# The scan's products of the state in two row halves of TensorE, and the first phase's steps in another order

## The chip, the cores and the metric

The kernel runs on one core of a Trainium2 chip. The metric is the device time of one execution in microseconds, the median of three runs. One more execution was recorded by the profiler; all durations below come from that one.

## What is computed

One decoder layer over 520 columns: 512 tokens of one prompt and 8 single new tokens of 8 running sequences. Differential attention (prompt tokens among themselves, new tokens against a paged cache) and an RWKV-7 time mixing run side by side, gates merge them, and a dense feed-forward network follows. The part that the change touches is the recurrence of the time mixing over the prompt, for 8 heads with a 64x64 state each:

```python
def step(S, inp):
    r_t, w_t, k_t, v_t, kk_t, a_t = inp
    sa = jnp.einsum("bhij,bhj->bhi", S, -kk_t)
    S = (S * w_t[:, :, None, :] + sa[..., None] * (kk_t * a_t)[:, :, None, :]
         + v_t[..., None] * k_t[:, :, None, :])
    return S, jnp.einsum("bhij,bhj->bhi", S, r_t)
S_fin, y = lax.scan(step, wkv0.astype(f32), seq)
```

## The kernel before

All activations stand with channels on the 128 partitions and the 520 columns along the free axis. A **first phase** computes all projections, the time mixing, both attentions, the gates and the merged product of both branches. A **second phase** (output projection and feed-forward network, tile `psW`) follows; no line of it is changed.

Dense products keep 32-bit accuracy by splitting: `whi` (ScalarE, ACT) and `wlo` (VectorE, DVE) are made from each loaded weight block `raw`, and TensorE (PE) runs three products per block into `psD`. An ordinary 32-bit product, such as those of the scan, appears in the trace as two matmuls, so 8 products are 16 matmuls there.

The recurrence is done in 16 **chunks** of 32 tokens (`scan_chain`, two chunks `e` per call `p`). A chunk takes the state `old`, a tile `STB` of 128 partitions: the 64 key channels of the even heads stand in the upper row half, those of the odd heads in the lower one, and four pairs of heads lie along the free axis. Its chain of work is:

1. 8 products of the state, one per head, of `WZ` (64 columns for each head: 32 for the solved keys, 32 for the receptance) with `old`, into one PSUM bank of the tag `P`, named `psC`. Here the contraction runs over all 128 partitions, and `WZ` holds zeros in the row half of the other head of the pair.
2. DVE adds `u0` to the first 32 rows and writes `uv`; ACT copies the other 32 rows to `yg`, the output.
3. 8 products of `bt` and `uv` (contraction over 64 rows, heads alternating between two column halves) into a second tile, also named `psC`.
4. DVE adds the decayed old state `SD` and writes the new `STB`, and makes the next `SD`.

Everything else of the scan hangs beside this chain: `scan_w` loads and computes `WZ` of the next pair of chunks, `scan_ak` and `scan_u0` make `u0`, `scan_post` (products `psR<-uv,G`) completes the output. `solve` inverts the 32x32 triangles on DVE; it borrows both `WZ` tiles for its result and its scratch, and sets their padding halves to zero on GpSimd (POOL) afterwards.

The order of the first phase is not the order of the code. Each operation is recorded as a numbered step (`Steps`), and the table `SEQ` lists the numbers in the order in which they are issued; this sets the order on every engine's queue and on the DMA queues (SP for weights, cache pages and constants, ACT for most others). `BUFS` gives the number of buffers of the shared pools: 35 of `T2` (SBUF, 520 columns) and 8 of `P` (one PSUM bank each, all 8 that there are).

Of the kernel before, what the change touches and what calls it, by code (L numbers as in the profile page):

```python
# [20 lines left out]
TP = 512  # L21
# [34 lines left out]
def host_consts():  # L56
# [41 lines left out]
BUFS = {"Q4": 4, "T2": 35, "raw": 2, "w": 2, "P": 8}  # L98
SEQ = """
    708 3 76 639 72 0 19 1873 14 73 9 5 1943 34 1874 24 39 29 642 2 4 63 1 71 640 65 64 643 77 67-68 62 20 641 57 22  # L100
    66 58 21 56 15 59 10 711 16 60 12 11 74 6 4445 35 7-8 36 644-655 25 136 61 13 40 26 17 669-680 41 30 18 27 31-32
    37 23 681-692 42 139 28 78 710 33 70 656-667 69 79 38 82-93 80 43 81 44 50 45 107-118 51 46 52 47 94-105 53 48
    75 54 49 55 119-130 668 138 140 693 106 694 141 695-698 142 131 700 144-155 699 143 133 701 134 132 169-180 135
    137 214 212 215 208 213 226 574 198 510 209 200 199 156-167 201 181-192 575 168 576 202 193 577 195 579-590 578
    203 197 287 227 196 702 194 604-615 429 222 591-602 511-512 616-627 603 703-704 216-219 628 228 629-630 229 210
    220-221 206 211 204 207 631 205 257-268 223 632 232-243 705 224 706-707 633 709 515-526 225 230 634 231 540-551
    635 288 1870 1867 636 244-255 513 637 514 638 269-280 256 349 552-563 281 289 283 290 282 527-538 284 564 419
    285 430 293-304 291 539 565 286 566 292 420 348 318-329 421-422 305-316 423 352 424 330-341 353 317 425 414-415
    342 350 426 344 567 351 343 409-410 416 345 417 427 418 354-365 712-713 568 1029 346 411 437 428 569 366-377 431
    413 412 434 570 432 478 433 379-390 571 347 378 572 391-402 436 714 573 715 1314 716 403 506 404 1312 405 1315  # L110
    998 717 996 1313 835 1013 999 1316 997 1011 1317 406 1000 718-729 1014 1318 1012 1001 407 1319 915 1002 1320 408
    1015 743-754 1321 1003-1005 1322 1006 1017 1323-1325 1007 730-741 1016 1008 1018 1326 1019 1030 1009 1020
    1327-1329 742 1010 1031 773 834 755-766 1330 435 1021 438 1034-1045 481 767 1032 769 1033 1059-1070 768 770 774
    771 916 905 1046-1057 772 836-837 906 1058 1028 1071-1082 907-908 900-901 909 1083 1085 840-851 910 838 911
    865-876 902 839 903-904 912 1084 1151 852-863 923 775 913 776 877-888 914 479 482 864 922 895-896 921 777 889
    779-790 1087 778 891 1086 897 1710 898 1088 804-815 899 893 890 917 892 918 791-802 919 1152 894 1153 816-827
    803 1181-1192 828 1154 830 1155 829 1022-1023 831 1090 1193-1204 1024 832 924 920 968 965 992 439-446 964
    925-932 1205 833 1221 1150 944-951 1206 1089 1362 447-454 967 963 952-959 455 933-940 960 458-465 457 966 456
    941 466-473 962 1156-1167 474 961 477 943 942 476 1168-1179 480 1091 475 483-486 1092 1713 488-491 1180 487
    1120-1131 1714 492 1207 1095-1106 493 1208-1210 986-989 1093 993 990 1094 974-977 991 994 1363 1132-1143 978 995  # L120
# [172 lines left out]
def body(ctx, tc, A):  # L293
# [396 lines left out]

    STB = [c1.tile([128, 4, 64], F32, name=f"STB{i}") for i in range(2)]

    WZ = [c1.tile([128, 2, 4, 2, 2, 32], F32, name=f"WZ{i}") for i in range(2)]

    def solve():
        au = TT.rearrange("p g h t -> p (g h) t")
# [732 lines left out]
```

## Time and profile before

| | |
|---|---|
| median of 3 runs | 934.95 us (933.47 to 935.07) |
| the profiled execution, its own time | 939.28 us |
| its span, first to last instruction | 937.5 us |
| PE busy | 902.8 us, 96% of the span |
| DVE busy | 566.7 us, 60% |
| ACT busy | 408.3 us, 44% |
| granted TensorE clock, mean | 0.996 |

PE is the busiest engine in every stretch. The first product of the first phase starts at 9.6 us, the first of the second phase at 511 us. Chunk 0 of the scan starts at 247 us, and the products of the state of the last chunk run at 383 us. A busy share of PE says that a matmul was in flight, and matmuls overlap: two that start 60 ns apart can each last 220 ns. So the cost of a group of matmuls is read from the time that the group occupies, not from the sum of durations.

### The profile page before, as it was taken

What the parts mean: (1) busy time and instruction counts of PE and PEld (TensorE: products, weight loads), DVE (VectorE), ACT (ScalarE), POOL (GpSimd) and SP (SyncE); (2) the same over time, 40 slices, a digit from 0 to 9 for tenths busy, and PEclk for the clock granted to TensorE, in tenths of its full rate; (3) what the DMA queues carried; (4) which work ended last, traced back from release to release, by engine and by line L of the source; (5) the groups of instructions that cost most, each with busy time, mean ns of one, the idle gap of its engine ahead of it and who ended that gap; (6) DMA issues with size and microseconds to landing.
All of it is one profiled execution on the core that took longest, in us unless ns stands there. A gap on an engine that the chain in (4) does not pass through costs nothing.

```text
span 937.5 us, 20851 instructions
## 1 busy us (share of the span) xinstructions
PE 902.8 (96%) x8419; PEld 846.2 (90%) x8419; DVE 566.7 (60%) x1179; ACT 408.3 (44%) x863; POOL 61.7 (7%) x85
## 2 busy tenths in 40 slices
PE   5999999989999989999999999999999999999998
PEld 5798989888786768789999999999999999999998
DVE  5467767778455797663467666566666655533332
ACT  8565455543465633313444446444444444322221
POOL 1000201100000177000000000000000000000000
PEclk9999999999999999999999999999999999999999
DMA  7132346745827777778963222222233222243432
GB/s 235 63 104 69 103 125 187 204 153 183 222 64 261 219 247 244 235 278 280 299 220 128 91 90 91 91 91 90 91 98 103 92 90 92 85 113 108 114 106 63
DMA packets 78867, 136.46 MB, mean 146 GB/s; under 512 B 20289, under 2 KB 33473, under 8 KB 78770
## 3 DMA queue, kind: packets, MB, share of 16 engines
q1 hardware_dynamic: 45438, 110.75, 37.0%
q10 hardware_dynamic: 33332, 24.38, 8.7%
q8 instruction: 66, 1.08, 0.5%
q14 instruction: 31, 0.25, 0.1%
HBM read 117.86 MB, written 17.23 MB: 144 GB/s over the span
## 4 chain that ended last, share of the span: by engine, by line
PE 75%; DMA 8%; DVE 2%; ACT 2%; SPq 1%; issue 1%; ACTq 1%; DVEq 0%
PE psW L277 45%; PE psD L277 21%; PE psR L277 4%; PE psB L277 2%; PE psA L277 2%; DMA vt<-cache_v 2%; DMA kt<-cache_k 2%; DMA raw<-w_in 1%; PE psC L277 1%; DVE wlo L277 1%; ACTq L277 1%; DMA raw<-w_pab 1%; DMA uv<-vtd 1%; SPq L1005 1%; ACT es L277 1%
## 5 line engine op out<-in xcount | busy, mean ns | idle before, releaser
L277 ACT CAST whi<-raw 128x512 fp32r<-128x512 f32 x252 | 154.0, 613 | 385.2 <-PE psW L277 240.0
L277 DVE TENSOR_TENSOR wlo<-raw,whi 128x512 fp32r<-128x512 f32 x252 | 174.1, 692 | 215.0 <-ACT whi L277 209.9
L277 PE MATMUL psD<-X,whi 128*128 128x260 f32 x1344 | 260.7, 294 | 9.8 <-ACT X L277 9.6
L277 PEld LDWEIGHTS psD<-X,whi 128*128 128x128 f32 x1344 | 211.3, 191 | 23.5 <-issue 9.7
L277 PE MATMUL psW<-F,whi 128*128 128x348 f32 (+1 forms) x1056 | 223.8, 320 | 0.0
L277 PE MATMUL psD<-X,wlo 128*128 128x260 f32 x672 | 191.9, 286 | 1.1 <-DVE wlo L277 0.9
L277 PEld LDWEIGHTS psW<-F,whi 128*128 128x128 f32 x1056 | 163.4, 188 | 0.1
L277 PE MATMUL psW<-F,wlo 128*128 128x260 f32 x704 | 140.4, 281 | 0.0
L277 PEld LDWEIGHTS psD<-X,wlo 128*128 128x128 f32 x672 | 128.2, 191 | 2.0 <-DVE wlo L277 1.9
L277 PEld LDWEIGHTS psW<-F,wlo 128*128 128x128 f32 x704 | 121.2, 188 | 0.3 <-DVE wlo L277 0.3
L277 PE MATMUL psW<-HH,whi 128*128 128x348 f32 x528 | 111.8, 320 | 0.0
L277 PEld LDWEIGHTS psW<-HH,whi 128*128 128x128 f32 x528 | 81.6, 188 | 0.0
L277 PE MATMUL psW<-HH,wlo 128*128 128x260 f32 x352 | 70.3, 280 | 0.0
L277 PEld LDWEIGHTS psW<-HH,wlo 128*128 128x128 f32 x352 | 60.7, 188 | 0.0
L277 PE MATMUL psW<-M,whi 128*128 128x348 f32 (+1 forms) x192 | 40.8, 320 | 0.6 <-ACT whi L277 0.6
L277 DVE TENSOR_TENSOR X<-psW,X 128x348 f32<-128x348 f32 (+1 forms) x64 | 24.3, 422 | 14.2 <-PE psW L277 14.1
L277 PEld LDWEIGHTS psW<-M,whi 128*128 128x128 f32 x192 | 29.7, 188 | 0.8 <-ACT whi L277 0.8
L277 PE MATMUL psW<-M,wlo 128*128 128x260 f32 x128 | 25.6, 281 | 0.0
L277 DVE TENSOR_TENSOR pc<-psD,RSTD 128x260 f32<-128x260 f32 x28 | 12.0, 427 | 20.1 <-PE psD L277 20.0
L277 PE MATMUL psB<-vt,ptm 128*8 128x128 f32 x512 | 17.0, 273 | 5.6 <-DMA vt<-cache_v 4.2
L277 PEld LDWEIGHTS psW<-M,wlo 128*128 128x128 f32 x128 | 22.1, 188 | 0.0
L277 PEld LDWEIGHTS psB<-vt,ptm 128*8 128x8 f32 x512 | 12.3, 89 | 9.5 <-DMA vt<-cache_v 6.2
(319 smaller groups left out, 1230.2 us busy)
## 6 DMA issues: line engine op xcount, KB each, us to landing
raw<-w_in SPq DMA_DIRECT2D x42, 512.0 KB, 4.4
kt<-cache_k SPq DMA_DIRECT2D x64, 256.0 KB, 4.0
vt<-cache_v SPq DMA_DIRECT2D x64, 256.0 KB, 3.6
raw<-w_gate SPq DMA_DIRECT2D x22, 512.0 KB, 3.2
raw<-w_up SPq DMA_DIRECT2D x22, 512.0 KB, 3.2
raw<-w_down SPq DMA_DIRECT2D x16, 512.0 KB, 3.4
gad<-gt ACTq DMA_DIRECT2D x16, 260.0 KB, 3.7
raw<-w_pab SPq DMA_DIRECT2D x8, 512.0 KB, 6.3
```

The costliest lines, as they stand in the source:

```text
L277: return self.steps.add(self.name, op, roots, lambda: getattr(self.eng, op)(*map(real, a), **{k: real(v) for k, v in kw.items()}))
L1005: return nc.sync.dma_start(out=t[:, i, :].get(), in_=src[bass.ds(v, 1)].rearrange("o p c -> (o p) c"))
```

## The change

The products of the state no longer contract over zeros. The even head of a pair is contracted over the upper 64 rows, the odd one over the lower 64 rows, each with its own part of `WZ`. They write the same 64 PSUM partitions, and for that the result `sc` now has two banks, one for each parity; these two banks are a tag of their own (`PP`, one buffer), and `P` goes from 8 buffers to 6. The two readers of `sc` go through both banks with a rearranged view (`by_half`).

`WZ` becomes one tile with two halves, one for each `p % 2`, of the size of one of the two tiles before. One DMA fills a half where two did; one ACT copy of 128 partitions takes the place of two of 64; the zeroing in `solve` is gone, and the scratch of `solve` is now a `T2` tile, of which there are 36.

The table `SEQ` is another one from its first entry on, and the order changes throughout the first phase.

```diff
-BUFS = {"Q4": 4, "T2": 35, "raw": 2, "w": 2, "P": 8}
+BUFS = {"Q4": 4, "T2": 36, "raw": 2, "w": 2, "P": 6}
 SEQ = """
-    708 3 76 639 72 0 19 1873 14 73 9 5 1943 34 1874 24 39 29 642 2 4 63 1 71 640 65 64 643 77 67-68 62 20 641 57 22
...
-    WZ = [c1.tile([128, 2, 4, 2, 2, 32], F32, name=f"WZ{i}") for i in range(2)]
+    WZ = c1.tile([128, 2, 4, 2, 2, 32], F32, name="WZ")
...
-        rr = WZ[1].rearrange("p a h e i t -> p (a h e i t)")
+        rr = WZ.rearrange("p a h e i t -> p (a h e i t)")
...
-        tmpr = WZ[0].rearrange("p a h e i t -> p (a h e i t)")
+        tmpr = T2("R", "tmpr")
...
-        for t in WZ:
-            for i in range(2):
-                pool.memset(t[64 * (1 - i):64 * (1 - i) + 64, i], 0.0)
...
-        wr = WZ[p % 2]
-        for i in range(2):
-            q = slice(64 * i, 64 * i + 64)
-            act.dma_start(out=wr[q, i].rearrange("p h e i t -> p h (e i t)"), in_=wrd[p, q])
+        wr = WZ[:, p % 2]
+        act.dma_start(out=wr.rearrange("p h e i t -> p h (e i t)"), in_=wrd[p])
...
-            for i in range(2):
-                q = slice(64 * i, 64 * i + 64)
-                act.copy(out=wr[q, i, :, e, 0, :], in_=ps[q])
+            act.copy(out=wr[:, :, e, 0, :], in_=ps)
...
-                sc = PS("C")
+                sc = late(psp, [128, 2, 512], F32, "PP", 1, "sc")
                 for h in range(8):
-                    pe.matmul(out=sc[r0:r0 + 64, h * 64:h * 64 + 64], lhsT=wr[:, h % 2, h // 2, e, :, :], rhs=old[:, h // 2, :],
+                    q, a = slice(64 * (h % 2), 64 * (h % 2) + 64), h // 2
+                    pe.matmul(out=sc[r0:r0 + 64, h % 2, a * 64:a * 64 + 64], lhsT=wr[q, a, e, :, :], rhs=old[q, a, :],
                               start=True, stop=True)
-                dve.tensor_tensor(out=uv[r0:r0 + 32, :TP], in0=sc[r0:r0 + 32, :], in1=u0[w0:w0 + 32, :], op=ALU.add)
-                act.copy(out=yg[b0 + 32 * e:b0 + 32 * e + 32, :TP], in_=sc[r0 + 32:r0 + 64, :])
+
+                def by_half(x):
+                    return x.rearrange("p (a b j) -> p b a j", b=2, j=64)
+
+                sv = sc[:, :, :256].rearrange("p b (a j) -> p b a j", j=64)
+                dve.tensor_tensor(out=by_half(uv[r0:r0 + 32, :TP]), in0=sv[r0:r0 + 32], in1=by_half(u0[w0:w0 + 32, :]), op=ALU.add)
+                act.copy(out=by_half(yg[b0 + 32 * e:b0 + 32 * e + 32, :TP]), in_=sv[r0 + 32:r0 + 64])
```

What the new order does to PE in the middle of the scan: a full chunk in the kernel before, from the products of the state (`psC<-STB,WZ`) over those of the step (`psC<-uv,bt`) to the next products of the state. `kt` are cache pages, `kA,qT` the scores of the prompt's attention.

```order
L277 MATMUL psC<-STB_107,WZ_109 64x64 x8
L277 MATMUL psB<-kt,QB 32x256 x16
L277 MATMUL psA<-kA,qT 128x512
L277 MATMUL psA<-kA,qT 128x128
L277 MATMUL psC<-uv,bt 64x64 x8
L277 MATMUL psA<-kA,qT 128x256 x2
L277 MATMUL psC<-STB_106,WZ_109 64x64 x8
```

And a full chunk of the changed kernel, on PE at about the same place in the scan (`psR` are the side products of the scan itself):

```order
L276 MATMUL sc<-STB_106,WZ 64x64 x8
L276 MATMUL psR<-uv,G 32x64 x24
L276 MATMUL psC<-uv,bt 64x64 x8
L276 MATMUL psR<-uv,G 32x64 x8
L276 MATMUL psR<-TT,AT 64x32 x16
L276 MATMUL psR<-ak,TT 32x64 x32
L276 MATMUL sc<-STB_107,WZ 64x64 x8
```

The chain's steps keep their sequence; what stands between them is other work, here that of the scan's own side products. Over the whole scan of the changed kernel, the products of the state of chunks 2 to 8 follow each other with nothing but such short groups between the chain's steps, and those of chunks 9 to 13 likewise; 72 matmuls of dense projections stand between these two runs. In the kernel before, those of chunks 4 to 10 follow each other in that way, and blocks of dense projections stand at six places between chunks 2 and 12.

On ACT's queue, in the scan of the kernel before, the load of one `WZ` tile, the copy of the output of a chunk, and the copies into the other `WZ` tile:

```order
L277 DMA WZ_109<-wrd 64x512 x2
L277 COPY yg<-psC 32x512
L277 CAST whi<-raw 128x512
L277 COPY es<-psA 128x256
L277 ACTIVATE qnt<-kA 128x512
L277 ACTIVATE nb<-mx 128x2
L277 COPY WZ_108<-psR 64x4x32 x2
```

The same on ACT's queue in the changed kernel:

```order
L276 COPY yg<-sc 32x2x4x64
L276 DMA WZ<-wrd 128x512
L276 DMA uv<-vtd 32x512
L276 DMA gad<-gt 128x520
L276 COPY ot<-psA 128x128
L276 DMA uv<-vtd 32x512
L276 CAST whi<-raw 128x512
L276 COPY WZ<-psR 128x4x32
```

One load takes the place of two and one copy that of two, and the copy of the chunk's output stands ahead of the load here.

## Rows read from the trace of the kernel before

**Rows 1.** Page, part 1: busy time and share of the span.

```profile
PE 902.8 (96%) x8419; PEld 846.2 (90%) x8419; DVE 566.7 (60%) x1179; ACT 408.3 (44%) x863; POOL 61.7 (7%) x85
```

**Rows 2.** Windows: from:to, length, busy by engine (count), clock, DMA share, GB/s.

```profile
9.50:511.00 501.50, 481.13 (x5455) 425.07 (x5455) 335.13 (x754) 242.03 (x543) 58.31 (x72) 0.99 0.59 187
247.00:347.00 100.00, 95.38 (x1646) 75.41 (x1645) 67.44 (x153) 55.74 (x156) 17.49 (x15) 1.00 0.62 193
511.00:933.00 422.00, 421.64 (x2964) 421.12 (x2964) 225.91 (x409) 157.55 (x309) 0.00 (x0) 1.00 0.30 95
```

**Rows 3.** Instructions by form, PE: rows*columns of the array, moving tile, count, mean ns.

```profile
L277 PE MATMUL psC<-STB,WZ 128*64 128x64 f32 x240 | 17.2, 225 | 0.1
L277 PE MATMUL psC<-uv,bt 64*64 64x64 f32 x256 | 11.2, 224 | 0.5 <-DVE uv L277 0.3
L277 PE MATMUL psR<-uv,G 64*32 64x64 f32 x256 | 8.7, 218 | 0.0
```

**Rows 4.** Timeline of one chunk, all engines: start, length in us, then the group.

```profile
248.75 0.42 DVE L277 COPY STB<-psC 128x256 f32<-128x256 f32 x1 [0.91 <-PE psC L277]
...
249.61 1.15 PE L277 MATMUL psC<-STB,WZ 128*64 128x64 f32 x16
...
250.79 0.69 DVE L277 TENSOR_TENSOR uv<-psC,u 32x512 f32<-32x512 f32 x1 [1.16 <-PE psC L277]
...
251.75 0.68 PE L277 MATMUL psC<-uv,bt 64*64 64x64 f32 x16
...
252.36 1.08 PE L277 MATMUL psR<-uv,G 64*32 64x64 f32 x32
...
252.47 0.43 DVE L277 TENSOR_TENSOR STB<-psC,SD 128x256 f32<-128x256 f32 x1
```

**Rows 5.** Timeline of PE, later in the scan.

```profile
290.49 1.02 PE L277 MATMUL psA<-ont,c_ones 128*128 128x512 f32 x2
...
295.78 1.34 PE L277 MATMUL psA<-kA,qT 64*128 64x512 f32 x4
...
301.61 0.86 PE L277 MATMUL psR<-uv,G 64*32 64x64 f32 x24
302.40 1.15 PE L277 MATMUL psC<-STB,WZ 128*64 128x64 f32 x16
...
311.31 0.64 PE L277 MATMUL psB<-kt,QB 128*32 128x256 f32 x8
311.87 1.15 PE L277 MATMUL psC<-STB,WZ 128*64 128x64 f32 x16
```

**Rows 6.** Waits of PE, the longest in total: us, times, longest.

```profile
PE psD L277 <- ACT X L277: 9.6, 1, 9.6
PE psA L277 <- DVE es L277: 5.1, 4, 2.4
PE psB L277 <- DMA vt<-cache_v: 4.2, 5, 2.1
PE psB L277 <- DVE KS L277: 1.7, 2, 1.0
```

**Rows 7.** Instructions by form, DVE and ACT: reads and writes in pieces, and `WZ`.

```profile
L277 DVE TENSOR_TENSOR STB<-psC,SD 128x256 f32<-128x256 f32 x15 | 6.3, 423 | 7.0 <-PE psC L277 6.9
L277 DVE TENSOR_TENSOR ar<-kk,e 128x256 f32<-128x256 f32 x8 | 3.3, 417 | 0.0
L277 ACT COPY WZ<-psR 64x128 f32<-64x128 f32 x32 | 8.1, 260 | 4.5 <-DVE gt L277 2.3 <-DMA WZ<-wrd 1.1 <-PE psR L277 0.7
L277 ACT COPY es<-psA 128x128 f32<-128x128 f32 x4 | 1.0, 248 | 0.0
L277 POOL MEMSET WZ<- 64x512 f32 (+2 forms) x6 | 3.1, 530 | 7.2 <-DMA td<-WZ 3.6 <-DVE WZ L277 3.6
```

**Rows 8.** Timeline of ACT: two copies of a chunk's output.

```profile
302.08 0.58 ACT L277 COPY yg<-psC 32x512 f32<-32x512 f32 x1 [6.77 <-DVE SD L277]
...
312.56 0.58 ACT L277 COPY yg<-psC 32x512 f32<-32x512 f32 x1
```

More of the change, by code (lines that the diff above doesn't have):

```diff
@@ new lines @@
+    3328 2941 3478-3485 3329 3561 2942 4151-4154 3486 3330 3615 3590-3593 3601 2943 3331 3498-3509 3487 3332 4155
+    2944 3510-3513 3440-3447 3333 3514 4156 3488-3495 3448 2945 4249 4293 1353 3600 4247 3334 2946 1836 3496
+    3449-3456 1354 2947 3335-3338 3799 3457 3497 3612 3704-3711 3341 3879 3654-3665 3342 3713 3712 3636-3647 1837
+    1355 3340 3666-3669 3714-3721 3339 1356 3648-3651 4438 3722 4157-4160 3670 1357 3724-3731 4161 3723 3671-3682
+    4362 3732-3733 4162 3683-3694 1358 3880 3616-3623 1359 3734-3741 3624 3695-3702 3742 3625-3632 3703 3743
@@ new lines @@
+    4421 4067-4074 3574-3585 3988 4075 4422 4076 3989 4077-4084 4370 4423 4371 3586 3990 3992-4003 4424 4085 3587
+    4425-4426 3991 4427-4434 4086 4577 4004-4015 4436 4440 4439 4017-4028 4016 4372 4384 4373 4634 4351 4087-4094
+    4633 3800 4443-4450 4095-4096 4453-4460 4471 3801 3768 4106-4117 3769 4385 4472 3770 3804-3815 4537 3771 4538
+    3829-3840 4386-4388 4463-4470 3802 4473-4480 4547 4118-4121 3803 4029-4040 4548 4122 4389 4295 4123 4742
+    3816-3827 4578 4374 4041 4124 4741 4042 3841-3852 4579 3828 4390 4375 4539-4546 4580 4125 4549-4556 4567
@@ new lines @@
+    4097-4104 4581-4593 4568 3853 4352 4105 4126 4771 4636 3854 4127 4391 4594-4605 4142 4353 4635 4827 4392
+    4559-4566 4828 4606 4354 4128 3958 4645 4129-4131 4646 4132 3343 4355 3959 3780 3344 3782 4133 4356 3956 3345
+    4393 3957 4569-4576 3346 4637-4644 3960 4656 3347 3781 3962 4357 4607-4618 4394 4655 3961 3783 4376 3349 4665
+    3963 4619-4630 3964 3784 4772 4666 3348 4358 3965 4647-4654 4774 4657-4664 4731 4773 4359 4134-4137 4775
+    3772-3775 4732 4776-4787 3350 4377 3351 4675 3352 4751 3966 4788-4799 4752 3353 3786 4631 4378 4138 3785
@@ new lines @@
+    4870 4398 2787 4869 2788 5127-5130 4399 4880 4400 2789 5133 4324 5131 4879 4401 2790 4325-4336 4890 4402
+    2791-2792 4403 4889 2793 4861-4868 4404 2794 4482 2795 4871-4878 4909 2796 4405 4899 4337-4348 4483 4900
+    4406-4408 4511-4522 4484 4349 4485 4350 4486-4497 4167 4523-4534 4910-4911 4881-4888 4535 4968 4891-4898
+    4965-4966 4901-4908 4967 4437 4498-4509 4977-4978 4939-4950 4510 4912 4988 4536 4913 4987 4914-4925 5047 4998
+    4951-4962 4168 4997 4169 4926-4937 4963 5146 5614 5153 5139 4172-4183 4938 4170 4964 4171 1360 2797-2800 1361
@@ new lines @@
+    4184-4195 3358 2801 2804 2803 4409-4412 2802 4196 4969-4976 4413 4415 4979-4986 5134 5007 4989-4996 4414
+    4999-5006 5135 5008 4197-4208 4416 5148 5017 5155 5018 5147 5136 5150 5048 5141 5028 5137 5154 5157 5049 5027
+    5143 5149 5140 5038 5156 5151 5077-5088 5142 5037 5158 5138 5144 5231 5052-5063 5152 5230 5159 5423 5145
+    5009-5016 5050 4209-4220 5051 5417 5089-5100 4221 3359 4222 3360 5019-5026 5101 5029-5036 5039-5046 5103-5106
+    3388-3399 5107-5108 5064-5075 5109-5111 3363-3374 5076 3361 5112 3362 5102 5113 5160 3400-3411 5609 5420
@@ L218 @@
+    5529-5540 5528 5196-5207 5541 5162 5542 5358 5297 5163 5209-5220 5543 5208 5353 5296 5544 5170-5181 5361 5221
+    5292 5360 5293 5183-5194 5182 5324-5335 5195 5290 5222 5291 5337-5348 5223 5336 5224 5545 5298-5309 5349
+    5356-5357 5311-5322 5310 5388-5399 5323 5354 5350 5355 5401-5412 5351 5400 5551 5352 5550 5362-5373 5413
+    5548-5549 5375-5386 5374 5553 5552 5593-5604 5387 5546 5414 5547 5580-5591 5415 5605 5416 5554-5565 5592
+    5567-5578 5566 5579 5606-5608"""
 class Late:
```

200 lines of the change are left out of this document (85 added, 115 removed).

## The prediction, made before the changed kernel was run

> **What bounds the kernel now.** The busy shares come first: PE has matmuls in flight for 96% of the span, the next engine is DVE with 60% [rows 1]. The windows then divide the run. From 511 us on, the second phase keeps PE busy in 421.64 of 422.00 us, and nothing of it is changed; so 422 us stand whatever happens. The first phase runs on PE from 9.5 to 511 us, with 481.13 of 501.50 us busy, which leaves 20.4 us of idle PE spread over it; in the 100 us that hold most of the scan PE is busy for 95.38, DVE for 67.44, ACT for 55.74 [rows 2]. The list of PE's waits says who makes the idle time: the input at the start (9.6 us, before that phase's first matmul), the prompt's softmax (`es`, 5.1), value pages (4.2), the new tokens' keys (1.7), and smaller ones [rows 6]. The chain of the scan is not among the long ones: before its products PE sat idle 0.1 and 0.5 us in total, over all 31 groups [rows 3]. So the scan is paid for as PE time, not as latency, and a matmul that leaves PE in the first phase takes its time with it, as long as the other work stays packed around it.
>
> **The products of the state.** They are 15 groups (chunk 0 has none) of 16 matmuls. In the timeline such a group occupies 1.15 us [rows 4, 5], 0.22 of it the length of the last matmul [rows 3]; the other 0.93 are 15 intervals of some 60 ns, one matmul after the other on all 128 rows. The neighbour in the chain, `psC<-uv,bt`, has as many matmuls with the same 64 moving columns, but contracts over 64 rows, and its heads alternate between two column halves: 16 matmuls in 0.68 us [rows 4]. There the halves run at the same time. The changed products alternate between two row halves instead. That row halves run together too is shown twice. `psR<-uv,G` alternates them: 32 matmuls in 1.08 us, 28 ns apart [rows 4]. And the attention's scores, whose halves write the same partitions in two banks exactly as the changed products will: four matmuls of 512 columns in 1.34 us, where two full-height matmuls of 512 columns that follow each other take 1.02 [rows 5]. I take the row of the same size, 0.68 us, so a group shrinks by 1.15 - 0.68 = 0.47 us, and 15 groups by **7.0 us**. Bounds: with the 28 ns of `psR<-uv,G`, 15 x 28 + 220 = 640 ns, a gain of 0.51 x 15 = 7.7 us; and nothing at all, if the halves took turns.
>
> [...]
>
> **The readers of the products.** DVE's addition (0.69 us) and ACT's copy (0.58 us) now read two banks in pieces of 64 elements [rows 4, 8]. No row has just that. The nearest: a DVE addition that writes pieces of 32 elements takes 417 ns for 256 elements, one that writes straight takes 423 [rows 7]. I take 0. Both ends: 0.1 us a chunk either way, and of that nothing on the path while other products stand between the steps, at most 1.5 us if all of it were.
>
> **One pair of banks, and six for the rest.** The next products of the state must wait until ACT has copied the output of the chunk before, which was not so with eight rotating banks. ACT is late at times: the copy that runs from 302.08 to 302.66 us ends after the next products began at 302.40, and the one at 312.56 ends at 313.14, with the next products at 311.87 [rows 5, 8]. With one pair these two would have cost 0.3 + 1.3 = 1.6 us. In the new order the copy can stand elsewhere in ACT's queue, so I take 0 and keep 1.6 as the upper end. For the other six banks: no long wait of PE names an engine that only had to empty a bank [rows 6]. I take 0; a loss cannot be excluded and goes into the slower rival.
>
> **The rest of the edits** lie off PE. ACT saves 16 copies: 32 of 260 ns become 16 of about 248 (the row of the same 128x128 shape), 8.3 - 4.0 = 4.3 us of an engine that idles half the time; POOL loses four memsets of the size of half a `WZ` tile that waited 7.2 us for the triangles, with nothing urgent behind them [rows 7]. The loads of `WZ` move the same bytes in half as many issues on ACT's queue. All are hidden by PE's work, which fills 95% of that stretch [rows 2]; if that cover were gone, they would be gains of at most 4.3 us, so 0 here too.
>
> **The new order** moves nearly every step of the first phase: what PE waits for at 20.4 us of places [rows 2] will be waited for elsewhere. The rows cannot say by how much. From both sides: all of the 20.4 us saved, or as much again lost. I take 0, since the work to be packed and its dependences are the same, and the order of before is packed to 96%.
>
> **The sum.** The profiled execution took 939.3 us (span 937.5). Minus 7.0 gives 932.3. The median of the plain runs, 934.95, lies 4.3 us below the profiled one; I carry that offset over: **928.0 us**, 0.75% less. A difference under 0.2%, 1.9 us, would not be told from no change.
>
> **Rivals.**
>
> *The order also closes waits.* If about half of PE's idle 20.4 us goes, 10 us come on top: 928 - 10 = 918. For it: the long waits (`es` 2.4 us at once, a value page 2.1) are single events that another neighbour on PE would cover [rows 6]. Against it: what closes one opens another.
>
> *The products don't get faster.* The two halves take turns, because the pair of a head writes the same partitions or because issue is the limit. Then the time stays at 935, give or take what the order does. [...]
>
> *The chain of the scan starves PE (slower).* The new order sets chunks 2 to 8 and 9 to 13 in two runs with only short groups between the steps. From the end of the state's products to the start of the step's, 0.99 us pass (250.76 to 251.75), 0.69 of it DVE's addition; from DVE's start on the step's products (248.75) to the state's next products (249.61) 0.86 us, 0.42 of it DVE's [rows 4]. What stands between must last as long. In the chunk of the changed kernel shown above, `psR<-uv,G` x24 is 48 matmuls, some 1.6 us at the pace of 32 in 1.08; elsewhere a seam has only `kt` x4, 0.64 us, with one or two matmuls beside it [rows 4, 5]. The two runs have 21 seams. To turn the gain of 7.0 us into a loss above 1.9, each would have to lose (7.0 + 1.9) / 21 = 0.42 us, by a short cover or by a bank not yet emptied. At 0.8 us lost in each, which is nearly the whole latency, it is 21 x 0.8 = 16.8 - 7.0 = 10 us more: 945. Against it: before, chunks 4 to 10 ran the same way, and PE's idle time in front of the chain's steps was 0.6 us in all [rows 3].
>
> **How the numbers follow.** The forecast gets 0.55, with its own range of 923 to 933 (the 7.7 us and some luck of the order below, the 1.6 and 1.5 us and some bad luck above). The order that also closes waits: 0.20, 908 to 923. No faster products: 0.10, 931 to 939. The starving chain: 0.15, 937 to 955. A range from 918 to 938 leaves out half of the second case and two thirds of the last, 2 in 10. Faster by more than 1.9 us: nearly all of the first, all of the second, a little of the third, 0.74. Within it: 0.11. Slower: 0.15.
>
> **What would show it.** In the profile of the changed kernel, `sc<-STB,WZ` should be 240 matmuls in groups of 0.65 to 0.70 us; 1.1 us would make the first step wrong and the second rival right. PE's busy time in the first phase should fall by about 7 us with its idle time near 20 us; idle time near 10 is the first rival. Waits of PE for `uv`, for `STB` or for ACT's `yg` that sum to several us, and more than 7, are the third. The second phase should take 422 us as before; if it doesn't, the premise that the first phase alone decides is wrong.

## The result, and the profile after

The changed kernel took 948.84 us (median of 4 runs, 942.08 to 951.81) against 935.01 us for the kernel before: ratio 1.0107, interval 1.0063 to 1.0151. It became slower by about 1%; the forecast was 928.0, the range 918 to 938. Two later measurements of the same kernel gave 942.12 us on chip 8 (ratio 1.0022, 0.9982 to 1.0062) and 944.59 us on chip 15 (1.0063, 1.0032 to 1.0095). So the size of the loss varies from measurement to measurement, but none shows the gain. (Executions that lie more than 1.5% above the fastest of their kernel are left out of the ratios, the mean clocks and the times at like clock, but not of the medians.)

The profiled execution took 946.65 us, its span is 944.9. Page, part 1, answers [rows 1]:

```profile
PE 912.6 (97%) x8419; PEld 852.0 (90%) x8419; DVE 566.0 (60%) x1179; ACT 405.6 (43%) x847; POOL 59.0 (6%) x81
```

PE has the same 8419 matmuls and was busy 9.8 us longer, not 7 us shorter. The windows say in which stretches (from:to, length, busy by engine and count for PE, PEld, DVE, ACT, POOL, then the granted clock, DMA share, GB/s); the first and the last line answer [rows 2]:

```profile
9.50:519.00 509.50, 491.16 (x5456) 431.18 (x5457) 334.61 (x755) 239.62 (x524) 55.98 (x68) 0.96 0.59 184
...
250.00:253.30 3.30, 1.07 (x9) 0.87 (x8) 0.00 (x0) 1.33 (x7) 0.00 (x0) 0.99 1.16 214
253.30:263.50 10.20, 9.36 (x64) 8.78 (x65) 2.74 (x7) 3.36 (x10) 0.00 (x0) 0.50 0.96 200
263.50:294.20 30.70, 29.32 (x612) 22.70 (x614) 14.41 (x31) 13.88 (x34) 0.00 (x0) 1.00 0.70 220
294.20:307.90 13.70, 13.70 (x251) 10.91 (x243) 4.16 (x9) 3.07 (x6) 0.00 (x0) 0.50 0.35 112
...
342.00:352.30 10.30, 10.30 (x143) 6.99 (x140) 3.24 (x6) 2.86 (x8) 2.19 (x2) 0.50 0.36 111
...
519.00:941.00 422.00, 421.44 (x2964) 420.85 (x2963) 225.89 (x410) 157.22 (x308) 0.00 (x0) 1.00 0.30 95
```

The second phase takes 422 us, as before. The first phase is 8 us longer. In three stretches of it, 34 us together, the granted clock is 0.50. Three more of 3.4 us each bring the sum to 44.4 us. The kernel before had two such stretches in its profiled run:

```profile
81.50:84.90 3.40, 3.40 (x18) 3.40 (x17) 1.04 (x4) 2.26 (x8) 0.00 (x0) 0.50 0.00 0
351.10:354.50 3.40, 3.40 (x35) 3.38 (x28) 2.71 (x8) 0.00 (x0) 2.35 (x2) 0.50 0.98 279
```

The books of the first phase: PE's idle time went from 20.4 to 18.3 us (509.50 - 491.16). Its busy time rose by 10.0 us (491.16 against 481.13). The products took about 7 us off, so something put about 17 us on. By an estimate from the granted clock of 0.50, the 37.6 us more at half clock (44.4 against 6.8) put on at most half their length, 18.8 us.

The groups by form answer [rows 3, 7], the timeline of PE answers [rows 4]; in the timeline a group at 289.5 us runs at full clock, one at 295.3 us at half:

```profile
L276 PE MATMUL sc<-STB,WZ 64*64 64x64 f32 x240 | 12.4, 255 | 0.0
L276 PE MATMUL psC<-uv,bt 64*64 64x64 f32 x256 | 12.9, 245 | 1.6 <-issue 1.4
L276 DVE TENSOR_TENSOR uv<-sc,u 32x512 f32<-32x512 f32 x15 | 10.3, 684 | 14.1 <-PE sc L276 8.1 <-ACT yg L276 5.8
L276 ACT COPY yg<-sc 32x512 f32<-32x512 f32 x15 | 8.7, 578 | 20.7 <-DVE uv L276 15.1 <-PE sc L276 5.4
L276 ACT COPY WZ<-psR 128x128 f32<-128x128 f32 x16 | 4.1, 267 | 7.8 <-PE psR L276 7.6
```

```profile
289.52 0.68 PE L276 MATMUL sc<-STB,WZ 64*64 64x64 f32 x16
...
291.60 0.44 PE L276 MATMUL psC<-uv,bt 64*64 64x64 f32 x7
293.42 0.45 PE L276 MATMUL psC<-uv,bt 64*64 64x64 f32 x9 [1.38 <-issue]
...
295.30 1.12 PE L276 MATMUL sc<-STB,WZ 64*64 64x64 f32 x16
```

The products of the state shrank from 1.15 to 0.68 us a group, to the hundredth as forecast. But from 294.2 us on the same group takes 1.12 us. Ahead of that fall PE stood still for 1.38 us in the middle of a group, waiting for nothing that the profile shows. The fall at 342.0 us follows a halt of the same kind, the one at 253.3 us a wait for ACT:

```profile
250.80 0.28 PE L276 MATMUL psD<-X,wlo 128*128 128x260 f32 x1
254.14 1.23 PE L276 MATMUL psA<-es,VT 128*128 128x128 f32 x4 [3.07 <-ACT es L276]
...
338.73 0.41 PE L276 MATMUL psR<-ak,TT 32*32 32x64 f32 x11
340.46 0.75 PE L276 MATMUL psR<-ak,TT 32*32 32x64 f32 x37 [1.33 <-issue]
```

ACT was late with `es` since one DMA issue stood on its queue for 4.00 us:

```profile
247.92 4.00 ACTq L276 DMA_DIRECT2D TT<-td  x1
```

The list of PE's waits answers [rows 6]; the chain of the scan (`uv`, `STB`, `yg`) is not among the long ones:

```profile
PE psA L276 <- ACT es L276: 3.3, 2, 3.1
...
PE psC L276 <- issue: 1.4, 1, 1.4
...
PE psR L276 <- issue: 1.3, 1, 1.3
```

### The profile page after: what moved, and what is told of

Same layout as the page of the kernel before. It is cut to its first block, busy times and chain, and to the rows that moved or that the text cites. A ratio compares the mean times of both kernels' runs of the same rounds, so it can differ in the third digit from the quotient of the medians.

```text
span 944.9 us, 20823 instructions
## 1 busy us (share of the span) xinstructions
PE 912.6 (97%) x8419; PEld 852.0 (90%) x8419; DVE 566.0 (60%) x1179; ACT 405.6 (43%) x847; POOL 59.0 (6%) x81
## 3 DMA queue, kind: packets, MB, share of 16 engines
q8 instruction: 66, 1.08, 0.5%
## 4 chain that ended last, share of the span: by engine, by line
PE 87%; DVE 4%; ACT 3%; DMA 2%; issue 1%; ACTq 1%; SPq 0%; DVEq 0%
PE psW L276 45%; PE psD L276 27%; PE psR L276 6%; PE psA L276 4%; PE psB L276 3%; DMA vt<-cache_v 1%; PE sc L276 1%; PE psC L276 1%; ACTq L276 1%; DVE wlo L276 1%; DVE es L276 1%; DMA TT<-gd 1%; ACT whi L276 1%; ACT es L276 1%; DMA td<-WZ 0%
## 5 line engine op out<-in xcount | busy, mean ns | idle before, releaser
L276 DVE TENSOR_TENSOR wlo<-raw,whi 128x512 fp32r<-128x512 f32 x252 | 177.2, 703 | 213.3 <-ACT whi L276 210.8
L276 PE MATMUL psD<-X,whi 128*128 128x260 f32 x1344 | 264.4, 297 | 12.8 <-ACT X L276 9.8
L276 PEld LDWEIGHTS psD<-X,whi 128*128 128x128 f32 x1344 | 214.2, 194 | 26.4 <-issue 11.0
L276 PEld LDWEIGHTS psD<-X,wlo 128*128 128x128 f32 x672 | 130.1, 194 | 0.5 <-DVE wlo L276 0.3
L276 DVE TENSOR_TENSOR gt<-psD,RSTD 128x260 f32<-128x260 f32 x32 | 13.6, 425 | 18.2 <-PE psD L276 17.9
L276 PE MATMUL psB<-kt,QB 128*32 128x256 f32 x256 | 20.5, 432 | 0.1
```

What stands on the lines that cost most here:

```text
L276: return self.steps.add(self.name, op, roots, lambda: getattr(self.eng, op)(*map(real, a), **{k: real(v) for k, v in kw.items()}))
```

## The experiments

**How times are compared.** Runs of one and the same kernel differ by up to 16 us, and nearly all of that goes with the mean granted clock: the kernel before took 930.6 to 946.5 us over 114 runs on five chips, at clocks of 1.0 to 0.984. So each kernel gets two numbers: its median, and its time at like clock. For the second, one slope was fitted to the time over the clock in 266 runs of 17 kernels, each with a level of its own. The slope is **8.2 us for 0.01 of mean clock** (interval 7.7 to 8.7); the level is the time that the line gives at clock 1.0. An estimate from the granted clock of 0.50 agrees: 0.01 of 940 us is 18.8 us at half clock, in which PE loses 9.4 us if it always has work.

| kernel | median, us (runs) | before on that chip | mean clock | at like clock 1.0 |
|---|---|---|---|---|
| before | 938.1 (117, all chips) | | 0.9937 | 932.8 ± 0.4 |
| changed, three measurements | 948.84, 942.12, 944.59 | 935.01, 937.71, 938.38 | 0.9838 | 930.1 ± 1.0 |
| e1 old order, halves | 941.17 (12) | 938.03 | 0.9853 | 929.4 ± 1.2 |
| e2, e15 new order, full height | 949.53 (4), 945.01 (12) | 938.03, 938.38 | 0.9875 | 935.5 ± 1.0 |
| e3 new order, halves and fillers | 958.61 (4) | 938.03 | 0.9858 | 945.8 ± 1.7 |
| e4 before, halt of 2.0 us | 946.00 (7) | 938.03 | 0.9861 | 935.5 ± 1.4 |
| e5 as e1, copy first | 940.10 (12) | 937.71 | 0.9879 | 930.6 ± 1.1 |
| e6 before, halt of 0.5 us | 939.42 (12) | 937.71 | 0.9943 | 933.9 ± 1.0 |
| e7 changed, half of the pages | 936.45 (10) | 937.71 | 0.9873 | 925.1 ± 1.2 |
| e9 as e5, full height | 942.22 (12) | 935.81 | 0.9901 | 934.2 ± 1.0 |
| e10 before, block of quarter products | 959.56 (4) | 935.81 | 0.9852 | 947.0 ± 1.8 |
| e11 before, block of full-height products | 950.99 (4) | 935.81 | 0.9932 | 945.3 ± 1.6 |
| e12 before, dense block | 951.08 (4) | 935.81 | 0.9942 | 946.5 ± 1.6 |
| e13 changed, `TT` loaded by POOL | 941.57 (12) | 938.38 | 0.9854 | 930.0 ± 1.2 |
| e16 as e10, half of the pages | 952.94 (6) | 938.20 | 0.9902 | 944.1 ± 1.4 |
| e17 as e11, half of the pages | 947.42 (6) | 938.20 | 0.9943 | 943.2 ± 1.3 |
| e18 before, half of the pages | 938.45 (12) | 938.20 | 0.9936 | 932.6 ± 1.1 |

The theories: **A**, the new order brings short halts of PE among small products, and a halt starts a stretch at half clock. **B**, the products in row halves lower the clock themselves; **B'**, the later form of it, says so of all products on a part of the array, halts or not.

### The two parts of the change apart

**e1: the old order, the products in row halves.** Results in two tiles of `P`, one per parity; the readers go through them in two pieces each.

```diff
-                sc = PS("C")
+                sc = [PS("C"), PS("C")]
...
-                    pe.matmul(out=sc[r0:r0 + 64, h * 64:h * 64 + 64], lhsT=wr[:, h % 2, h // 2, e, :, :], rhs=old[:, h // 2, :],
+                    q, a = slice(64 * (h % 2), 64 * (h % 2) + 64), h // 2
+                    pe.matmul(out=sc[h % 2][r0:r0 + 64, a * 64:a * 64 + 64], lhsT=wr[q, h % 2, a, e, :, :], rhs=old[q, a, :],
```

> The products of the state in two row halves and two banks, in the order of the kernel before (the two banks are taken from the common pool of eight; for that DVE's addition and ACT's copy are done in two pieces). Theory A (the new order makes the clock fall): groups of 0.68 us, clock 0.99 or more, about 7 us less than before minus up to 2 for the split readers: 928 to 932. Theory B (the half-height products make it fall): falls of the clock in the scan, between 247 and 385 us, mean clock 0.98 or less, 938 or more.

Measured: 941.17 us, ratio 1.0043 (1.0018 to 1.0067): not faster either. The clock fell at 299.8 us for 17 us, right behind a halt that the pieced copy brought (timeline of PE, then the window of the fall):

```profile
299.18 1.12 PE L277 MATMUL psC<-STB,WZ 64*64 64x64 f32 x16 [0.95 <-ACT yg L854]
```

```profile
299.80:316.90 17.10, 15.96 (x177) 9.28 (x174) 9.70 (x28) 8.49 (x27) 0.00 (x0) 0.50 0.53 154
```

**e2: the new order, every product over all 128 rows** (here `WZ` holds no zeros, so each product sums over both heads of its pair and the values are not the recurrence's; only the work is the same).

```diff
-                    pe.matmul(out=sc[r0:r0 + 64, h % 2, a * 64:a * 64 + 64], lhsT=wr[q, a, e, :, :], rhs=old[q, a, :],
+                    pe.matmul(out=sc[r0:r0 + 64, h % 2, a * 64:a * 64 + 64], lhsT=wr[:, a, e, :, :], rhs=old[:, a, :],
```

> The changed kernel in its new order, but each product of the state contracts over all 128 rows again (without the padding zeros, so the sum mixes both heads of a pair: only the time is to be read). Theory A: the clock still falls in the scan, mean 0.97 to 0.98, groups of 1.15 us, 945 to 958. Theory B: mean clock back at 0.99 or more, 930 to 938.

Measured: 949.53 us, ratio 1.0106 (1.0058 to 1.0154), the same as the changed kernel's first measurement. So the new order alone is slower than before by as much. Four runs could not say what the halves bring beside it, so it was run again later, beside the changed kernel (e14) and on one chip.

> The changed kernel beside e13 and e15 on one chip. Both theories: median 940 to 949 us, clock 0.980 to 0.987 in the mean of the runs.

> e2 again, the new order with products over all 128 rows and nothing else changed, beside e14. If the row halves bring their 7 us of PE time also in the new order: 5 to 7 us above e14 at like granted clock. If the clock takes back what they bring (theory B'): the mean clock of e15 is higher than that of e14 by 0.003 or more and the medians lie within 3 us of each other.

Measured on that chip, means of the runs: before 938.7 us at a mean clock of 0.9928, new order with full height 944.2 at 0.9897, changed kernel 944.0 at 0.9828. With the levels at like clock (from these runs alone) every step divides into work and clock:

| step | at like clock | clock | by the clock, at 8.2 us per 0.01 | sum |
|---|---|---|---|---|
| new order | +3.0 ± 1.2 us | -0.0031 ± 0.0033 | +2.5 | +5.5 |
| row halves | -5.9 ± 1.6 us | -0.0069 ± 0.0042 | +5.6 | -0.2 |

The row halves bring nearly what was forecast, and the clock takes it back. That is the outcome written down for B'. Over all runs of both kernels the halves' part of the clock is smaller and not apart from nil, -0.0037 ± 0.0040; that of the work stays, -5.4 ± 1.1 us. The new order's part of the clock is there the larger one, 0.9875 against 0.9937, and clear of nil (-0.0062 ± 0.0035).

The profile of e15 shows a place of the new order, far ahead of the scan, where the clock fell (timeline of PE, then the window):

```profile
33.24 2.87 PE L276 MATMUL psR<-m,c_a2p 64*128 64x8 f32 x12
```

```profile
36.20:53.30 17.10, 17.10 (x28) 6.76 (x29) 0.55 (x1) 8.79 (x14) 0.00 (x0) 0.50 0.07 26
```

PE had no halt between 27.3 us and the fall, and the DMA engines were nearly idle (0.07). The same group, of 2.87 us each time, stands in all eight profiles of kernels in the new order. In three of them (e2, e3, e15) 13.7 to 17.1 us at half clock follow it; in the other five the clock stays at full speed there. No profile of a kernel in the old order has a fall ahead of 78 us. So the order can bring falls that have nothing to do with the scan's products, and it does not in every run.

### What starts a stretch at half clock

**e3: the changed kernel, with eight dense matmuls of 256 columns behind every group of products.**

```diff
+                        if h == 7:
+                            for k in range(8):
+                                i = nc.tensor.matmul(out=real(sc)[:, k % 2, 256:512], lhsT=real(XHI)[:, k, 0:128],
+                                                     rhs=real(XHI)[:, k, 0:256], start=True, stop=True)
```

> The changed kernel with 8 additional full-height matmuls of 256 columns behind each of the 15 groups of products of the state, into unused columns of the same banks: some 0.9 us of PE each at full clock, 13 us in all. Theory A: the fillers keep the clock up in the scan (mean 0.985 or more), so that the time rises by less than the 13 us, or falls: 938 to 950. Theory B: the half-height products are all still there, the clock stays at 0.975, and the time is 13 us or more above the changed kernel: 960 or more.

Measured: 958.61 us, between what the two theories had named. The fillers cost more than they save (15.7 us at like clock), but in the profiled run the scan kept the full clock from 273 us to the end of the phase:

```profile
273.00:511.00 238.00, 233.17 (x3397) 201.99 (x3390) 144.81 (x311) 92.24 (x211) 38.41 (x28) 1.00 0.72 235
```

Both halts on issue were gone as well, so this run does not tell a halt from the small products. Nor does the mean clock of its four runs, 0.9858, stand apart from the changed kernel's 0.9838: the profiled one lost 13.7 us to the half clock at 37.4 us, where no filler stands.

**e4 and e6: the kernel before, with 4 or 2 additions on DVE ahead of chunk 7's new state**, that is a longer wait of PE at one place and nothing else.

```diff
+                    if c == 7:
+                        for _ in range(4):
+                            nc.vector.tensor_tensor(out=real(st["abase"]), in0=real(st["abase"]), in1=real(st["abase"]), op=ALU.max)
```

> The kernel before, with four additions of 0.69 us each put on DVE ahead of the new state of chunk 7, in its longest run of chunks without dense projections: PE should stand still for about 2 us near 302 us. Theory A, that one stall among small products starts a fall of the clock that lasts until dense work returns (318 us in that order): clock 0.5 for about 7 to 14 us, and 5 to 9 us more than before, several times the stall. If stalls don't matter: 2 to 3 us more, clock 0.996.

> The kernel before, full-height products, with two additions on DVE (1.0 us) ahead of chunk 7's new state, half of e4's four. Theory A: PE halts about 1 us at 301 us; if a halt of that length is enough, the clock falls to one half until about 319 us as in e4, and the time is 7 to 8 us above before (ratio about 1.008). If the fall needs the longer halt, or needs half-height products beside it (theory B), the clock stays at 1.0 there and the time is 0 to 1.0 us above before (ratio 1.000 to 1.001).

Measured: 946.00 us (ratio 1.0097, 1.0065 to 1.0130) and 939.42 us (1.0000, 0.9969 to 1.0031). The timeline of e4, with the window of the fall, then that of e6:

```profile
301.96 1.94 PE L277 MATMUL psC<-STB,WZ 128*64 128x64 f32 x16 [2.00 <-DVE STB L854]
```

```profile
301.90:319.00 17.10, 17.04 (x169) 11.80 (x173) 8.58 (x23) 7.66 (x23) 0.00 (x0) 0.50 0.49 125
```

```profile
303.99 1.12 PE L277 MATMUL psC<-STB,WZ 128*64 128x64 f32 x16 [0.55 <-DVE STB L854]
...
309.40 1.15 PE L277 MATMUL psC<-STB,WZ 128*64 128x64 f32 x16
...
314.24 1.97 PE L277 MATMUL psC<-STB,WZ 128*64 128x64 f32 x16 [1.24 <-ACT yg L277]
```

A halt of 2.00 us cost 8 us in the median: 2 of it are the halt, the rest is the clock (0.0076 lower in the mean, 6.2 us), as in the 17 us at half clock behind it, in which PE was busy for 17.04 us. A halt of 0.55 us, less than the 1 us that was aimed at, started nothing: the next group ran at full clock, and the clock fell only behind another halt, of 1.24 us, for one short stretch. So in the old order, with full-height products, one halt of 2.00 us among small products was enough to lower the clock for 17.1 us, and the one of 1.24 us came ahead of 3.4 us. That is A, and the longer halt cost four times its own length.

**e5 and e9: e1 without its halt, with and without the row halves.** In e5, ACT copies chunk 7's output ahead of the two loads of `WZ` that had held the copy up. e9 is e5 with `lhsT=wr[:, h % 2, a, e, :, :], rhs=old[:, a, :]`, so over all rows.

> The old order with products in row halves, as in e1, but on ACT the copy of chunk 7's output stands ahead of the two loads of WZ that held it up by 1.2 us in e1 (the only change against e1). Theory A (a halt of PE among small products starts a stretch at the half clock that lasts until dense products return, and that eats the gain): the halt of 0.95 us at about 298 us is gone, the stretch of 17 us at half clock at 300 us with it, and the time falls below the kernel before by up to the 7 us of the products: ratio 0.992 to 0.996. Theory B (half-height products among small ones lower the clock by themselves): the halt goes but the clock still falls near 300 us; ratio 1.002 to 1.006 as in e1.

> The old order as in e5 (copy of chunk 7's output ahead of the loads of WZ, results in two tiles, readers in two pieces each), but every product again over all 128 rows. Only the row halves separate it from e5. Theory B' (products that use half the rows or a quarter of the array lower the clock, halts or not): the clock is that of the kernel before, about 0.993, against 0.988 in e5, and the time is 937 to 940, no better than e5, because the 7 us of the products are back. Theory A (halts start the falls): the halts that the split readers bring are as in e5, so the clock stays near 0.988 and the time is 4 to 7 us above e5, 944 to 947.

Measured: e5 940.10 us (1.0026, 0.9995 to 1.0057), e9 942.22 us (1.0055, 1.0025 to 1.0085). The fall at 300 us was gone from e5, but another followed 6 us later, behind a page that came 2.21 us late:

```profile
305.15 0.64 PE L277 MATMUL psB<-kt,QB 128*32 128x256 f32 x8 [2.21 <-DMA kt<-cache_k]
...
306.52 1.12 PE L277 MATMUL psC<-STB,WZ 64*64 64x64 f32 x16
```

At like clock the halves gain 3.6 ± 1.3 us here (930.6 against 934.2). Each theory had a part wrong. Removing the halt did not bring the gain of A. And the clock of e9, 0.9901 with full height, is neither the 0.993 of B' nor the 0.988 of A: what e9 shares with e5 (readers in pieces, two banks, the moved copy) costs clock already, and the row halves at most a little more, 0.0022 ± 0.0022.

**e7 and e8: the changed kernel without every second load of key pages, and as it is.**

```diff
-            kt = load_pages(A["cache_k"], b, 2 * (n // 2), "kt").rearrange("p a (h t) -> p a h t", h=4)
+            if b % 2 == 0:
+                kt = load_pages(A["cache_k"], b, 2 * (n // 2), "kt").rearrange("p a (h t) -> p a h t", h=4)
```

> The changed kernel, but the key pages of every second sequence are not loaded (the products use the pages of the sequence before, so the scores of the new tokens are not computed rightly): half of that traffic is gone from the scan. If the two halts of 1.4 us inside product groups that PE's records put down to issue (292 and 339 us) come from instruction packets that wait for the crowded DMA engines: both halts shrink below 0.5 us, the stretches at half clock at 294 and 342 us go, and the time falls by about 12 us to near 937. If they come from the number of instructions alone: both halts stay at 1.2 us or more, and the time stays within 3 us of the changed kernel (about 949).

> The changed kernel as it is, beside the others on one chip. Both theories: 946 to 951 us, mean granted clock 0.974 to 0.987.

Measured: 936.45 us and 942.12 us (the second below the 946 to 951 expected). The halts on issue were gone from e7, and so was the wait for `es` at 251 us. So these halts go with the crowded DMA engines (a busy share of 0.82 in 288 to 294 us and of 0.92 in 334 to 341 us of the changed kernel), not with the number of instructions alone. But the clock fell all the same. The windows and the timeline of e7 around it:

```profile
250.00:280.70 30.70, 30.70 (x540) 24.71 (x538) 15.83 (x35) 14.84 (x38) 0.00 (x0) 1.00 0.63 186
280.70:291.00 10.30, 10.30 (x188) 7.57 (x189) 2.30 (x5) 2.02 (x7) 0.00 (x0) 0.50 0.48 159
```

```profile
278.77 0.68 PE L276 MATMUL psC<-uv,bt 64*64 64x64 f32 x16
279.38 0.44 PE L276 MATMUL psR<-uv,G 32*32 32x64 f32 x16
279.75 0.92 PE L276 MATMUL psR<-TT,AT 32*64 32x32 f32 x32
280.60 2.12 PE L276 MATMUL psR<-ak,TT 32*32 32x64 f32 x64
```

PE was busy in all of the 30.70 us ahead of the fall. What it did last were groups on a quarter of the array or less: 64 rows by 64 columns, then 32 by 32 and 32 by 64. So a halt is not needed: against A. e18, the kernel before with the same pages left out, is the base for the time (it is told with e16 below). At like clock e7 is **7.4 ± 1.5 us faster** than e18 (925.1 against 932.6); that is the row halves and the new order together. With the halts gone the whole forecast gain is there. The clock of e7 is still 0.0063 ± 0.0036 lower, which is worth 5.2 us.

**e13: the changed kernel, the four loads of `TT` issued by POOL.** This takes away the one halt whose cause is on a queue.

```diff
-                act.dma_start(out=TT[r0:r0 + 32].rearrange("s g h t -> s (g h) t"), in_=td[u0:u0 + 32].rearrange("u s t -> s u t"))
+                pool.dma_start(out=TT[r0:r0 + 32].rearrange("s g h t -> s (g h) t"), in_=td[u0:u0 + 32].rearrange("u s t -> s u t"))
```

> The changed kernel, with the four loads of TT from td issued by POOL instead of ACT; one of them held ACT's queue for 4.0 us at 248 us, and PE then waited 3.07 us for es. Theory A (halts start the falls): the halt at 251 us shrinks below 1 us, the stretch at half clock behind it goes, and the time falls by 3 us for the halt and 2 to 5 us for the clock: 5 to 8 us below the changed kernel on this chip. Theory B' (the runs of small products lower the clock, whatever the halts): the halt goes and with it 2 to 3 us, the falls between 280 and 345 us stay, the mean clock stays within 0.003 of the changed kernel's.

Measured: 941.57 us against 944.59 for the changed kernel on that chip, clock 0.9854 against 0.9828. From the timeline and the windows of e13:

```profile
247.74 3.29 POOL L276 DMA_DIRECT2D TT<-td  x4 [13.05 <-DVE es L276]
...
251.94 0.61 PE L276 MATMUL psA<-es,VT 128*128 128x128 f32 x4
```

```profile
253.30:263.50 10.20, 8.74 (x157) 6.33 (x159) 1.31 (x3) 4.58 (x12) 0.00 (x0) 1.00 1.02 257
288.90:305.90 17.00, 16.61 (x272) 12.29 (x274) 4.61 (x9) 3.65 (x7) 0.00 (x0) 0.50 0.34 102
```

The halt and the stretch at half clock behind it are gone, and a fall at 288.9 us stands later in the scan, behind another halt on issue. The time moved by 3 us, not by 5 to 8, and the clock by 0.0026: the outcome of B'. The interval of the clock's difference (± 0.0039) holds nil as well, and the means over all twelve runs of each are 944.04 and 944.01 us, so the 3 us of the medians are not a gain that is shown. At like clock the two kernels are the same, 930.0 and 930.1 us.

### A block of one kind of product, by itself

**e10, e11, e12: the kernel before, with a block of extra matmuls in a row ahead of chunk 8's products**: 320 on a quarter of the array, 192 of full height with the same 64 moving columns, or 112 dense ones. The results go to unused columns.

```diff
+                        if c == 8 and h == 0:
+                            for i in range(160):
+                                k, j0 = i % 8, 64 * (i % 2)
+                                nc.tensor.matmul(out=pc[j0:j0 + 64, 256 + 64 * (k // 2):320 + 64 * (k // 2)], lhsT=bt[r1:r1 + 64, k * 64:k * 64 + 64],
+                                                 rhs=uv[r1:r1 + 64, k * 64:k * 64 + 64], start=True, stop=True)
```

> The kernel before, with 160 more products of bt and uv (320 matmuls of 64 rows by 64 columns, 64 moving columns, two column halves in turn, as psC<-uv,bt has them) in one block without a halt ahead of chunk 8's products of the state; results go to unused columns. At full clock the block lasts about 12 us. Theory B': the clock falls inside the block although PE never stops, and stays low until dense products come back; the block takes up to 24 us and the time is 18 to 26 us above before. Theory A: no halt, no fall; 12 us above before, 949 to 951.

> As e10, but the block consists of 96 more products of the state over all 128 rows (192 matmuls of 128 rows by 64 columns, 64 moving columns), about 12.9 us at full clock. Theory B': the clock falls less than in e10 or not at all; the time is 13 to 17 us above before. Theory A: 13 us above before, as no halt is added.

> As e10, but the block consists of 112 dense matmuls (bf16, 128 by 128, 256 moving columns), about 12.0 us. Both theories: no fall inside the block, 12 us above before, 948 to 951. Theory B' further: no stretch at half clock for the 20 us behind it either.

Measured: 959.56, 950.99 and 951.08 us. The timelines of e10, then e11, then e12:

```profile
303.12 4.17 PE L842 MATMUL psC<-uv,bt 64*64 64x64 f32 x135
308.44 9.70 PE L842 MATMUL psC<-uv,bt 64*64 64x64 f32 x185 [1.16 <-issue]
318.08 1.97 PE L844 MATMUL psC<-STB,WZ 128*64 128x64 f32 x16
```

```profile
301.74 11.41 PE L842 MATMUL psC<-STB,WZ 128*64 128x64 f32 x192
```

```profile
302.46 13.52 PE L841 MATMUL psC<-X 128*128 128x256 f32 x112
```

At full clock the blocks last 9.6 (the quarter products, in e16 below) to 13.5 us. Only within the quarter products did the clock fall, from 309.0 to 336.3 us:

```profile
309.00:336.30 27.30, 27.30 (x356) 21.16 (x350) 9.34 (x24) 8.17 (x24) 0.00 (x0) 0.50 0.22 68
```

The time, 23.8 us above before, is what B' had asked for. But a halt on issue of 1.16 us stood in that block, where the DMA engines were busy with pages. Two of the four runs of e10 lie at clocks of 0.990 and 0.992, two at 0.980 and 0.979. So the block was put where no such halt should come.

**e16, e17, e18: the quarter block, the full-height block and no block, all with half of the key pages.**

> e10's block (320 matmuls of 64 rows by 64 columns, about 10 us at full clock) in the kernel before, but without the key pages of every second sequence (the scores of the new tokens are not computed rightly), so that no halt should stand in the block. Theory B' (products on a quarter of the array lower the clock): the clock falls inside or right behind the block in the profile though PE doesn't stop, and the mean clock of the runs is 0.004 or more below that of e17. Theory A (only halts start falls): no fall there, mean clocks within 0.002 of e17 and e18, and the time about 10 us above e18.

> e11's block (192 full-height matmuls of 128 rows by 64 columns, 11.4 us) with the same half of the page traffic. Both theories: no fall inside the block, mean clock as e18, the time about 11.4 us above e18.

> The kernel before with half of the page traffic and no block, as the base of the two. Both theories: mean clock 0.993 to 0.997; the time 0 to 6 us below the kernel before, since the waits for pages go.

Measured: 952.94, 947.42 and 938.45 us. The block of e16 now ran without a halt, at full clock to its end:

```profile
307.09 9.55 PE L842 MATMUL psC<-uv,bt 64*64 64x64 f32 x320
316.57 1.15 PE L844 MATMUL psC<-STB,WZ 128*64 128x64 f32 x16
```

That is against B': 9.55 us of nothing but quarter products did not lower the clock in this run, neither inside nor behind. The mean clock of e16's six runs is 0.0042 ± 0.0052 below that of e17; B' had asked for 0.004, but the interval holds nil. Nor can it be put down to the block: the profiled run has its long stretch at half clock 49 us ahead of it, with PE busy throughout:

```profile
240.80:257.90 17.10, 17.10 (x183) 13.37 (x181) 4.78 (x10) 5.26 (x15) 0.00 (x0) 0.50 0.51 166
```

A block of the still smaller products that came last ahead of e7's fall (32 rows by 32 or 64 columns) was not run. At like clock e18 is as fast as the kernel before (932.6 against 932.8), so there the page traffic costs the old order nothing, and the new one 4.9 ± 1.2 us (e7 against the changed kernel).

**What stands, and what stays open.** Shown: at like clock the changed kernel takes less time than the one before (930.1 against 932.8 us), and its lower clock costs more than that (8.1 us). Behind a halt of 2.00 us among small products stood 17.1 us at half clock, behind one of 0.55 us none (e4, e6). Such a stretch also started without any halt, after 30.70 us of busy PE in e7 and 8.9 us in e15, and small products did not always bring it (the 9.55 us of e16, and five of the eight profiles of the new order at 36 us). Once low, the clock stayed low with PE busy throughout for 10.3 us (e7) to 27.3 us (e10). Not settled: what makes the clock fall in one run and not in the next, and whether the row halves lower it in the new order on every chip. No version that computes the same values beats the kernel before: the best of them by work, e13, e5 and e1 at 929 to 931 us at like clock, give it back through the clock.

## Why the prediction was wrong

**The bound and the second phase** were right: 421.44 of 422.00 us [rows 2].

**The products of the state** were right in mechanism and in size: 0.68 us a group against 1.15 [rows 4], in the layout of two row halves and two banks. The 7.0 us came as 5.9 ± 1.6 (e14 against e15), and as 7.4 ± 1.5 together with the new order where no halts disturbed it (e7 against e18). The rival in which the halves take turns, or issue is the limit, did not come: 16 matmuls of the changed products took 0.68 us, and the block of e16 ran 320 in 9.55 us, 30 ns each.

**The readers** at 0 were right: 684 and 578 ns, with the pieces as without [rows 4, 8]. **The pair of banks** was right too: PE waited 0.0 us ahead of `sc`. So were **the edits off PE**: the copies of `WZ` fell from 8.1 to 4.1 us on ACT [rows 7].

**The new order** at 0 was wrong, inside the ends that were given: at like clock it costs 3.0 ± 1.2 us. The rivals had looked for this in the chain of the scan. The runs point elsewhere: half of the page traffic took 4.9 ± 1.2 us off the changed kernel (e7), and the halts on no semaphore and the wait for `es` went with it. The DMA issue that blocked ACT's queue is not shown to cost anything by itself: without it the time at like clock is the same (e13).

**The step that failed** is the premise that "a matmul that leaves PE in the first phase takes its time with it". At like clock it nearly held: 5.9 ± 1.6 of the 7.0 us came. The profile before showed a mean clock of 0.996, and the prediction used it neither as a term nor as a rival. The rows gave little warning: the run of chunks 4 to 10 was already mostly small products, and the 100 us around it had a granted clock of 1.00 [rows 2]; only that mean and the 0.99 of the whole first phase told that the clock can fall at all. The mean clock went from 0.9937 to 0.9838; at 8.2 us per 0.01 that is 8.1 us, more than the whole gain. In these terms the change reads: 932.8 - 5.4 (halves) + 2.7 (order), both at like clock, give 930.1; 8.2 us per 0.01 below clock 1.0 add 13.3 for the changed kernel and 5.2 for the one before: 943.4 against 938.0, the means of their runs. Levels and slope come from those same runs, so that this closes is no proof; the sizes of the terms are what it tells. What lowers the clock in either part of the change stays open.

**The rival of the starving chain** had named 945 us, close to what came, but for another reason: PE never waited long for `uv`, `STB` or `yg`. **The sign to look for** that the prediction gave, busy time of PE down by 7 us with idle time near 20, tells the two apart: idle was 18.3 us, busy time rose by 10.0. **The offset** of 4.3 us between the profiled and the plain runs lies within the spread of one kernel's runs, 930.6 to 946.5 us. The profiled run of the kernel before also lies 3.2 us above the line of like clock and that of the changed kernel 4.0 us below it, so the books of these two are not those of the average run. **The range** was a little worse covered than its sum says: of the starving chain's 937 to 955 nearly all lies above 938, not two thirds, so it left out some 24 in 100 and not 20.

## What to carry to other kernels

Where PE is the bound, price a change to it twice: the time of its matmuls at full clock, and what the granted clock will do; list the stretches at half clock before and after, and compare kernels at like clock, since a run tells its clock. A halt of PE can cost several times its length: one of 2.00 us, with small products behind it, cost 8 us in e4. Among dense products the price was smaller: near 190 us of the old order, halts of 1.83 to 2.79 us came ahead of 3.4 us at half clock in e9, e10 and e12, and halts of 2.39 to 2.44 us ahead of none in the kernel before, e6 and e11. So dense blocks are best kept where PE may wait. The changed kernel, whose order packs small products into long runs, looked better at like clock than in its plain times: with half of the pages left out of both, it was 7.4 us ahead of the kernel before at like clock and 2.0 us by the medians (e7 against e18).

## What the runs showed of the hardware

- The clock stayed at half with PE at work: PE was busy for 27.30 of 27.30 us at a granted clock of 0.50 (e10) and for 17.04 of 17.10 (e4). Dense products did not lift it at once: in e16 those of `psD` fill most of 240.8 to 245.9 us, and the clock stayed at half until 257.9.
- PE halted in the middle of a group of like matmuls with no semaphore to wait for that the profile shows: for 1.16 us in e10, 1.33 and 1.38 in the changed kernel, 1.93 in e13. In the changed kernel and in e13 it halted at the same matmul, after 7 of 16 of one `psC<-uv,bt` (1.38 and 1.93 us). With half of the page traffic they were gone from e7 and from the block of e16. The page of the changed kernel has a DMA queue of the kind `instruction` (66 packets, 1.08 MB in the run, so 16 KB each), with one packet in 288 to 294 us; that PE waited for it was the author's guess, and is not shown.
- One issue of the load of `TT` stood on ACT's queue for 4.00 us (247.9 to 251.9 us, at a DMA share of 1.01); the four issues of that load took POOL 3.29 us together (e13).
- Matmuls of 64 moving columns followed each other at 30 ns where they alternated between two column halves (320 in 9.55 us, e16), at 59 ns over all 128 rows (192 in 11.41 us, e11).
